# Other places in SBUF for the split weights and the tiles around them

## The chip, the cores and the metric

The kernel runs on one core of a Trainium2 chip. The metric is the time of one execution on the device in microseconds (us): the median of the runs is 1040.94 us before the change (three runs, 1040.69 to 1042.45).

The engines are named as the profile names them: PE (TensorE, matmuls), PEld (its loading of weights), DVE (VectorE), ACT (ScalarE), POOL (GpSimd), SP (SyncE, here an issuer of DMAs).

## What is computed

One layer of a bidirectional encoder: batch 1, sequence 512, width 1024, all in float32. The condition `c` gives nine vectors of shifts, scales and gates.

```python
h = modulate(rmsnorm(x, norm_ffn1), sh1, sc1)
x = x + 0.5 * g1 * swiglu(h, w_ffn1_in, w_ffn1_out)      # FFN1, inner width 2816

h = modulate(rmsnorm(x, norm_mix), sh2, sc2)
qa, ka, va, qb, kb, vb, ga, gb = split(h @ w_in)
ya = window_gqa_sink(rope(qa), rope(ka), va) @ w_branch_a  # 8 heads of 64, 2 of keys, window 128
yb = diff_attention(rope(qb), rope(kb), vb) @ w_branch_b   # 4 heads, two softmaxes each
merged = sigmoid(ga) * ya + sigmoid(gb) * yb
x = x + g2 * (merged @ w_out)

h = modulate(rmsnorm(x, norm_ffn2), sh3, sc3)
x = x + 0.5 * g3 * swiglu(h, w_ffn2_in, w_ffn2_out)      # FFN2
```

## The kernel before

**Three products for one.** A float32 operand is split into a high part, rounded to the type fp32r, and a low part, the rest. A product of two split operands is three matmuls that add up in one bank of PSUM: high by high, high by low, low by high (`mm3`; `two` in the FFNs; L173 to L175 and L456 to L458 in the profile). Each matmul has two operands in SBUF: the **weights**, 128 by 128, which PE loads ahead (PEld), and the **moving** operand, 256 or 512 columns that are streamed past the weights. A row of the profile or of the order of instructions names the tile it writes, an arrow, the moving operand, and the weights: `acc<-b,high` streams an activation in a tile `b` past weights in the tile `high`.

**The stages**, with their times in the profiled execution: the condition, the first norm and a first part of FFN1 (to 82 us), FFN1 (82 to 339 us), the gates of the mixers (to 377 us, and on beside other work), projections and the two attentions (377 to 644 us), the branches and the output product (644 to 729 us), FFN2 (729 to 1038 us). Most of the FFNs' input products are made by `Unit`s: a scheme of Strassen's kind, with seven products, named `a11`, `s1`, `a12`, `a22`, `s4`, `s2` and `s3`, where others would need eight. Each is a group of 24 matmuls or multiples of it with 256 columns. In most groups the moving operand lies in a tile `b`; for `s1` it lies in a tile `u` (rows `acc<-u,low`).

**The places.** Split weights come to lie in two large tiles, `high` and `low`, each with five places of 1024 floats (`HILO`), handed out in turn by `high_low`. The start of a place is `i * 1024 + min(i, 2) * GAP + aside` floats: only the first two places have a gap of 64 floats (256 bytes) behind them, and `aside` shifts the operand inside its place by `ASIDE` (16 floats, 64 bytes), `TURN` (24 floats, 96 bytes), `FAR` (64 floats) or nothing, as the caller asks. The other tiles (`b8`, of which `b` in the profile are parts, `u4`, named `u`, `ka`, `x`, `raw`, `f2`) are laid out in the order in which the kernel first asks for them, so that a small tile ahead of them shifts them.

**What the text counts.** While a matmul streams its moving operand, PE loads the weights of the next one. The *offset* of a pair is the address of the next matmul's weights less that of the current moving operand, modulo 256 bytes. It can be read from the places: `high` begins at 64 modulo 256, `b8` at 64 and `u4` at 160. With `ASIDE` the weights lie at 128, so that a tile `b` gives 64 and a tile `u` gives 224; with `TURN` and a tile `b` it is 96.

**The order of instructions.** The order on each engine is a list scheduler's, which works from modelled costs and sees when an operation overwrites what another still reads; a few stretches are written by hand (`tc.manual_schedule`, `in_order`, `issue_after`). Weights come by DMA, most from SP's queue and a part from POOL's, are split by ACT (the high part) and DVE (the low part), and are then read by PE.

Of the kernel before, what the change touches and what calls it, by code (L numbers as in the profile page):

```python
# [13 lines left out]
I32 = mybir.dt.int32  # L14
# [82 lines left out]

RAW, HILO, F2 = 5, 5, 8

ASIDE, TURN, GAP = 16, 24, 64  # L100

FAR = 64


BRANCH_ASIDES = (ASIDE, TURN, ASIDE, ASIDE), (ASIDE,) * 4
MIX_ASIDES = 0, 0, 0, 0, 0, 0, ASIDE, ASIDE

CHUNKS = (range(0, 6), range(6, 12), range(12, 16), range(16, 22))
# [25 lines left out]
def layer(ctx: ExitStack, tc: tile.TileContext, a: dict):  # L134
# [13 lines left out]
    def xt():  # L148
        return sbuf("x", [P, T], F32, 8)
# [16 lines left out]
    def keep(shape, nm, dt=F32):  # L166
        return sb.tile(shape, dt, name=nm, tag=nm, bufs=1)
# [28 lines left out]
    def high_low(n=1024, aside=0, holder=None):  # L196
        while turn[0] % HILO in holders:
            turn[0] += 1
        i = turn[0] % HILO
        turn[0] += 1  # L200
        if holder:
            holders[i] = holder
        i = i * 1024 + min(i, 2) * GAP + aside
        return tuple(t[:, i : i + n] for t in parts)

    def let_go(holder):
# [24 lines left out]
    sub8, lam_s, nlam = (keep([P, n], nm) for nm, n in (("sub8", 1), ("lam_s", 2), ("nlam", 1)))  # L231
    rqa, ccol = keep([P, NT, 8], "rqa"), small(NC)
    x = [xt() for _ in range(NC)]
    parts, modv = [], []
    for nm, n in (("high", 6), ("low", 0)):
        parts.append(keep([P, HILO * 1024 + 2 * GAP + ASIDE], nm, F32R))
        modv += [keep([P, NC], f"mod{v}") for v in range(n)]

    def load_by(t, src, n):
# [9 lines left out]
        return w  # L249


    begin, begins, norms = keep([P, 6 * NC], "begin"), {}, {SC1: NORM1, SC2: NORM2, SC3: NORM3}

    def mod_begin(v):
        if v in (SH1, SH2, SH3):
# [204 lines left out]
    class Unit:  # L460
# [12 lines left out]
        MAKE = {"s1": 5, "a11": 3, "a12": 2, "s2": 4, "s4": 2, "s3": 2, "a22": 3}  # L473
        asked, length = ("s1", "a11", "a12", "a22"), 1.0

        in_order = turned = ()
        spare, roomy, apart, more = ("s1",), (), (), {"s1": ("s2", "a11"), "s2": ("s4", "a12"), "a11": ("s3", "a21")}

        def place(self, q):
# [14 lines left out]
        def prepare(self, q):  # L494

            if q in self.ready:
                return
            self.ask(q)
            n = self.depth * 2 * P
            if q in self.apart:  # L500
                both = b8().rearrange("p a b -> p (a b)")
                hi, lo = both[:, 0:n], both[:, 1024 : 1024 + n]
            else:
                hi, lo = high_low(n, TURN if q in self.turned else ASIDE, (self, q))
            t = self.at[q]
            with tc.issue_after(copied[0]) if q in self.in_order and copied else nullcontext():
                split_from(hi, lo, t)
            self.ready[q] = hi, lo
            if q in self.more:
                s, src = self.more[q]  # L510
                G.dma_start(t, self.srcs[src], accum_op=ALU.add)
                self.at[s] = t
# [102 lines left out]
    cact = [sbuf("ka", [P, D], F32, 1)]  # L615
    hh, hl = new_h()
    modv += [keep([P, NC], f"mod{v}") for v in range(len(modv), 9)]
    nc.scalar.dma_start(ccol, a["c"])
    tc.keep_in_program_order(nc.scalar.dma_start(par, a["par"]))
    for c in range(NC):  # L620
# [2 lines left out]
    with tc.manual_schedule(engines=BOUND | {mybir.EngineType.SP, mybir.EngineType.Pool}):  # L623
# [24 lines left out]
        def first_loads(k):  # L648
            n = 1 if k else 2
            scale = mod_load(SC1, k, n=n)  # L650
            if k == 0:
                kept.append(keep([P, NT], "pos", I32))
            shift = mod_load(SH1, k, n=n) if k == 0 else None
            raw = sbuf("raw", [P, 1024], F32, RAW)
            load_by(raw, a["w1s"][k], n)
            w1[k] = [scale, shift or mod_load(SH1, k), raw]
# [227 lines left out]
    def in_unit1(p):  # L884
        srcs = {q: a["w1u"][p - PLAIN, i] for i, q in enumerate(("a11", "a12", "a21", "a22"))}
        u = Unit(srcs, 4, h1_operand, in_post1, p % 2)
        u.p, u.in_order = p, ('s2', 's4')
        return u

    class Out1:  # L890
# [17 lines left out]
        def prepare(self, m):  # L908
            if m not in self.ready:
                self.ask(m)  # L910
                aside = FAR if not self.by_halves(m) else TURN if m < NC - LAST_1 + 2 else ASIDE
                if self.final and m == 0:
                    while turn[0] % HILO != 1:
                        turn[0] += 1
                t = self.ready[m] = high_low(self.depth * P, aside, (self, m))
                with tc.issue_after(copied[0]):
                    split_from(*t, self.at[m])
# [279 lines left out]
    def project_pairs(srcs, then):  # L1197

        n = 2 * P
        out = [bank("acc") for _ in range(2)]  # L1200
        for u, src in enumerate(srcs):
            wh, wl = load_main(src, ASIDE)
            for t in range(NT):
                ht = slice(t * P, (t + 1) * P)
                po = out[t // 2][:, t % 2 * n : (t % 2 + 1) * n]
                for i in range(4):
                    k = 4 * u + i
                    w = slice(i * n, (i + 1) * n)
                    first, last = k == 0 and t % 2 == 0, k == NC - 1 and t % 2 == 1
                    PE.matmul(po, hh[k][:, ht], wh[:, w], start=first, stop=False, skip_group_check=True)  # L1210
                    PE.matmul(po, hh[k][:, ht], wl[:, w], start=False, stop=False, skip_group_check=True)
                    PE.matmul(po, hl[k][:, ht], wh[:, w], start=False, stop=last, skip_group_check=True)
                    yield MM3 / 2
        then(out)
# [11 lines left out]
    def gates(more=lambda: True):  # L1226
        while gate_next[0] < 16 and more():
            j = gate_next[0]
            gate_next[0] += 1

            wh, wl = load_main(a["w_gate"][j], ASIDE * (j == EARLY_A))
            out = bank("acc")
            for k in range(NC):
                o = k * P
                mm3(out, wh[:, o : o + P], wl[:, o : o + P], hh[k], hl[k], k == 0, k == NC - 1)
                yield MM3
            gate_end(j, out)
# [423 lines left out]
            turns["w"] = (b, g * nk + kc + 1)  # L1661


    def branch(w, j0, o_h, o_l, then, load, r=FULL[0], asides=(0, 0, 0, 0)):
        for u in range(4):
            with tc.issue_after(banded_last[0]):
                wh, wl = load(w[u], aside=asides[u])
            for i in range(2):
                j = 2 * u + i
                g = f2()[:, r]  # L1670
                nc.sync.dma_start(g, gate_scr[j0 + j][:, r])
                y = bank("acc")[:, r]
                for k in range(4):
                    o = k * 256 + i * P
                    mm3(y, wh[:, o : o + P], wl[:, o : o + P], o_h[:, k, r], o_l[:, k, r], k == 0, k == 3)
                    yield MM3 * (r.stop - r.start) / T
                then(j, g, y, r)

    def main():
        yield from beside(project(vb_w, T, values_b), LATER)  # L1680
        yield from beside(project(a["w_kb"], T, keys_b), LATER)
        yield from beside(project(a["w_qb"], T, queries_b), LATER)
        yield from beside(gates(lambda: gate_next[0] < EARLY_A), 1)
        while later or asked:
            column(later)
        tables_a()
        yield from project_pairs([a["w_kva"][u] for u in range(2)], keys_a)
        for g in range(2):
            yield from project_pairs([a["w_qa"][2 * g + u] for u in range(2)], lambda ps, g=g: queries_a(ps, g))
        yield from gates(lambda: done["b"] < NT)  # L1690
        line.drain(lambda: done["b"] == NT)
        start_a()
        yield from gates()
        ma = [b8(F32) for _ in range(2)]

        def then_a(j, g, y, r):
            V.scalar_tensor_tensor(ma[j // 4][:, j % 4, r], g, 1.0, y, ALU.add, ALU.mult)
            line.helped(0.6)

        yield from branch(a["w_yb"], 8, ob_h, ob_l, then_a, load_main)  # L1700
        mix.extend(new_h())
        mh, ml = mix

        def then_b(j, g, y, r):
            V.scalar_tensor_tensor(g, g, 1.0, y, ALU.add, ALU.mult)
            m = ma[j // 4][:, j % 4, r]
            V.tensor_tensor(m, m, g, ALU.add)
            split_from(mh[j][:, r], ml[j][:, r], m)
            line.helped(1.0)

        for i, r in enumerate(HALVES):
            line.drain(lambda: done["a"] >= 2 * i + 2)
            yield from branch(a["w_ya"], 0, *wa["o"], then_b, load_halves, r, BRANCH_ASIDES[i])

    mix = []
    line.run(main())
# [45 lines left out]

    def in_unit(p):
        srcs = {q: a["w2i"][p, i] for i, q in enumerate(("a11", "a12", "a21", "a22"))}
        return Unit(srcs, 4, h_operand, in_post, p % 2)


    act = {}
# [71 lines left out]
            V.scalar_tensor_tensor(g, g, -1.0, self.bank[1, t], ALU.mult, ALU.mult)  # L1840

    plain = units[0] = Plain(units[0].srcs, 4, h_operand, None, 0)
    plain.turned = ("a11", "a21")
    lead = units[1]
    lead.spare, lead.roomy, lead.apart = ("s1", "a11", "a12"), ("a22",), ("s1", "a12")
    for u in units[1:]:
# [254 lines left out]
```

## Time and profile before

| | before |
|---|---|
| median of three runs | 1040.94 us |
| the profiled execution: its span | 1039.1 us |
| DVE busy | 787.7 us, 76% |
| ACT busy | 583.8 us, 56% |
| DMA moved | 220.92 MB |

The span reaches from the first instruction to the last; the median lies 1.84 us above it. Matmuls are pipelined: the profile gives a matmul from the start of its stream to its modelled end, so that a matmul of 256 columns shows some 0.28 us while the next one starts 0.11 us after it. A difference of a few nanoseconds between two rows of matmuls of one shape is a difference in the distance from start to start:

```profile
start us, us, engine line op out<-in xcount [idle before <-releaser]
652.75 0.28 PE L175 MATMUL acc<-b,low 128*128 128x256 f32 x1
652.86 0.28 PE L173 MATMUL acc<-b,high 128*128 128x256 f32 x1
652.97 0.28 PE L174 MATMUL acc<-b,high 128*128 128x256 f32 x1
653.09 0.28 PE L175 MATMUL acc<-b,low 128*128 128x256 f32 x1
```

The columns are the start, the duration, the engine, the line and the operation.

### The profile page before, as it was taken

How to read it: one execution, taken by the hardware profiler on the slowest of the kernel's cores; microseconds unless marked ns; L12 is line 12 of the kernel's file. 1: busy time of each engine (PE TensorE's matmuls, PEld its weight loads, DVE VectorE, ACT ScalarE, POOL GpSimd, SP SyncE). 2: the span in 40 equal slices, each digit the busy share in tenths (PEclk: the TensorE clock that was granted, in tenths of full speed). 3: DMA queues.
4: the chain of work that ended last, by engine and by line, in shares of the span. 5: the costliest groups of instructions: out<-in, count | busy, mean ns of one | idle time of the engine just before them, and what ended most of it. 6: DMA issues, size and time to landing. Idle time of an engine off the chain costs nothing.

```text
span 1039.1 us, 18835 instructions
## 1 busy us (share of the span) xinstructions
PE 1031.4 (99%) x7346; PEld 952.4 (92%) x7346; DVE 787.7 (76%) x1456; ACT 583.8 (56%) x1014; POOL 162.9 (16%) x190
## 2 busy tenths in 40 slices
PE   9999999999999999999999999999999999999998
PEld 7789899899998998899888888989999999999998
DVE  7786667567796679859772588976899777877867
ACT  6665335244465343667785856525867546655553
POOL 1101110110110100543333101001112112212210
PEclk9999999999999999999999999999999999999999
DMA  9978787967884359796737944974498998989974
GB/s 363 358 233 203 234 231 212 257 160 221 237 203 138 146 201 410 234 286 138 182 71 190 263 129 158 359 248 102 97 237 193 246 225 207 230 221 216 206 149 112
DMA packets 69225, 220.92 MB, mean 213 GB/s; under 512 B 8336, under 2 KB 11024, under 8 KB 69136
## 3 DMA queue, kind: packets, MB, share of 16 engines
q1 hardware_dynamic: 46656, 146.52, 38.8%
q0 software_dynamic: 19344, 68.70, 36.3%
q10 hardware_dynamic: 3136, 4.51, 1.2%
q8 instruction: 57, 0.93, 0.3%
q14 instruction: 32, 0.26, 0.1%
HBM read 209.46 MB, written 10.23 MB: 211 GB/s over the span
## 4 chain that ended last, share of the span: by engine, by line
PE 94%; DMA 2%; DVE 2%; ACT 2%; issue 0%; SPq 0%; DVEq 0%; ACTq 0%
PE acc L457 7%; PE acc L456 7%; PE acc L458 7%; PE sc L456 6%; PE sc L457 6%; PE sc L458 6%; PE sc L173 5%; PE sc L174 5%; PE sc L175 5%; PE acc L173 5%; PE acc L175 5%; PE acc L174 5%; PE tp L1269 2%; DMA raw<-w1s 2%; PE acc L1193 2%; PE acc L1191 2%
## 5 line engine op out<-in xcount | busy, mean ns | idle before, releaser
L189 ACT CAST high<-raw 128x1024 fp32r<-128x1024 f32 (+2 forms) x176 | 158.4, 913 | 150.7 <-PE sc L174 41.1
L189 DVE TENSOR_TENSOR low<-raw,high 128x1024 fp32r<-128x1024 f32 (+2 forms) x176 | 183.5, 1052 | 40.2 <-ACT high L189 38.7
L456 PE MATMUL acc<-b,high 128*128 128x256 f32 x508 | 140.9, 277 | 0.0
L457 PE MATMUL acc<-b,high 128*128 128x256 f32 x508 | 140.8, 277 | 0.1
L458 PE MATMUL acc<-b,low 128*128 128x256 f32 x508 | 140.6, 277 | 0.0
L457 PE MATMUL sc<-b,high 128*128 128x256 f32 x500 | 138.2, 276 | 0.0
L456 PE MATMUL sc<-b,high 128*128 128x256 f32 x500 | 138.2, 276 | 0.0
L458 PE MATMUL sc<-b,low 128*128 128x256 f32 x500 | 138.2, 276 | 0.0
L189 ACT CAST high<-u 128x1024 fp32r<-128x1024 f32 (+1 forms) x73 | 75.5, 1035 | 52.6 <-PE sc L174 20.2
L189 DVE TENSOR_TENSOR low<-u,high 128x1024 fp32r<-128x1024 f32 (+1 forms) x73 | 87.7, 1202 | 21.3 <-ACT high L189 19.6
L173 PE MATMUL sc<-b,high 128*128 128x512 f32 (+1 forms) x272 | 97.5, 358 | 0.0
L174 PE MATMUL sc<-b,high 128*128 128x512 f32 (+1 forms) x272 | 97.1, 357 | 0.0
L175 PE MATMUL sc<-b,low 128*128 128x512 f32 (+1 forms) x272 | 97.1, 357 | 0.0
L457 PEld LDWEIGHTS acc<-b,high 128*128 128x128 f32 x508 | 95.5, 188 | 0.4 <-DVE b L1885 0.3
L456 PEld LDWEIGHTS acc<-b,high 128*128 128x128 f32 x508 | 95.5, 188 | 0.3 <-ACT f L533 0.2
L458 PEld LDWEIGHTS acc<-b,low 128*128 128x128 f32 x508 | 95.4, 188 | 0.0
L456 PEld LDWEIGHTS sc<-b,high 128*128 128x128 f32 x500 | 93.9, 188 | 0.0
L458 PEld LDWEIGHTS sc<-b,low 128*128 128x128 f32 x500 | 93.9, 188 | 0.0
L457 PEld LDWEIGHTS sc<-b,high 128*128 128x128 f32 x500 | 93.9, 188 | 0.0
L173 PE MATMUL acc<-b,high 128*128 128x512 f32 (+1 forms) x240 | 89.0, 371 | 0.0
L175 PE MATMUL acc<-b,low 128*128 128x512 f32 (+1 forms) x240 | 86.7, 361 | 0.0
L174 PE MATMUL acc<-b,high 128*128 128x512 f32 (+1 forms) x240 | 86.6, 361 | 0.0
(397 smaller groups left out, 2720.6 us busy)
## 6 DMA issues: line engine op xcount, KB each, us to landing
u<-w_mod SPq DMA_DIRECT2D x38, 512.0 KB, 8.1
b<-w_mod SPq DMA_DIRECT2D x32, 512.0 KB, 5.7
raw<-w2i SPq DMA_DIRECT2D x31, 512.0 KB, 5.4
u<-w2i POOLq DMA_DIRECT2D x31, 512.0 KB, 7.4
raw<-w1u SPq DMA_DIRECT2D x24, 512.0 KB, 6.4
u<-w1u POOLq DMA_DIRECT2D x24, 512.0 KB, 6.6
raw<-w1o SPq DMA_DIRECT2D x24, 384.0 KB, 4.9
raw<-w_gate SPq DMA_DIRECT2D x16, 512.0 KB, 5.4
```

Of the source, the lines that this page charges most:

```text
L173: PE.matmul(out, wh, xh, start=first, stop=False)
L174: PE.matmul(out, wh, xl, start=False, stop=False)
L175: PE.matmul(out, wl, xh, start=False, stop=last)
L189: last = S.copy(hi, src), V.tensor_tensor(lo, src, f(hi), ALU.subtract)
L456: PE.matmul(out, wh[:, s], xh, start=first and j == 0, stop=False, skip_group_check=True)
L457: PE.matmul(out, wh[:, s], xl, start=False, stop=False, skip_group_check=True)
L458: PE.matmul(out, wl[:, s], xh, start=False, stop=last and j == 1, skip_group_check=True)
L1191: PE.matmul(out[t][:, 0:n], hh[k][:, ht], wh[:, o : o + n], start=k == 0, stop=False)
L1193: PE.matmul(out[t][:, 0:n], hl[k][:, ht], wh[:, o : o + n], start=False, stop=k == NC - 1)
L1269: PE.transpose(tp[:, j * P : (j + 1) * P], src, ident)
```

## The change

No operation of the computation is added or removed. The start of a place becomes `i * (1024 + GAP) + ASIDE + aside`: every place has a gap of 64 floats behind it, and all of them are shifted by 64 bytes. Callers that want something else ask for it: `s1` of the `Unit`s takes no shift of its own (`asides`), the projections take `-ASIDE`. `TURN` and all its uses go. Two small tiles (`pad1`, 192 bytes, and `pad2`, 96 bytes), 16 more floats in `begin` and a larger `pos` shift the tiles behind them. The ring for DMAs that POOL issues shrinks from 4096 to 2048 bytes.

```diff
-ASIDE, TURN, GAP = 16, 24, 64
+ASIDE, GAP = 16, 64
...
-        i = i * 1024 + min(i, 2) * GAP + aside
+        i = i * (1024 + GAP) + ASIDE + aside
...
+    keep([P, 48], "pad1")
...
-        parts.append(keep([P, HILO * 1024 + 2 * GAP + ASIDE], nm, F32R))
+        parts.append(keep([P, HILO * (1024 + GAP) + ASIDE], nm, F32R))
...
-    begin, begins, norms = keep([P, 6 * NC], "begin"), {}, {SC1: NORM1, SC2: NORM2, SC3: NORM3}
+    begin, begins, norms = keep([P, 6 * NC + ASIDE], "begin"), {}, {SC1: NORM1, SC2: NORM2, SC3: NORM3}
...
-                hi, lo = high_low(n, TURN if q in self.turned else ASIDE, (self, q))
+                hi, lo = high_low(n, self.asides.get(q, ASIDE), (self, q))
...
+    keep([P, 24], "pad2")
...
-        u.p, u.in_order = p, ('s2', 's4')
+        u.p, u.in_order, u.asides = p, ('s2', 's4'), {"s1": 0}
...
-                aside = FAR if not self.by_halves(m) else TURN if m < NC - LAST_1 + 2 else ASIDE
+                aside = ASIDE if self.by_halves(m) else FAR
...
-            wh, wl = load_main(src, ASIDE)
+            wh, wl = load_main(src, -ASIDE)
...
-            wh, wl = load_main(a["w_gate"][j], ASIDE * (j == EARLY_A))
+            wh, wl = load_main(a["w_gate"][j])
...
-            yield from branch(a["w_ya"], 0, *wa["o"], then_b, load_halves, r, BRANCH_ASIDES[i])
+            yield from branch(a["w_ya"], 0, *wa["o"], then_b, load_halves, r, ASIDE)
...
+        u.asides = {"s1": 0}
...
-    plain.turned = ("a11", "a21")
...
-    nc = bacc.Bacc("TRN2", target_bir_lowering=False, num_devices=1, dynamic_dma_scratch_size=4096)
+    nc = bacc.Bacc("TRN2", target_bir_lowering=False, num_devices=1, dynamic_dma_scratch_size=2048)
```

The tiles then begin, modulo 256 bytes: `high` and `low` at 0 (before 64), `u4` at 0 (160), `raw` at 64 (192), `f2` at 64 (192); `b8`, `ka` and `x` stay at 64. Counted over all pairs of matmuls that follow one another, by the columns of the first and the offset:

| columns | offset | before | after | which ones |
|---|---|---|---|---|
| 256 | 64 | 3864 | 4944 | most of the FFNs; after, also the projections, `s1` and the attentions' `op<-u,b` |
| 256 | 224 | 458 | 0 | `s1` of the `Unit`s |
| 256 | 96 | 330 | 0 | the first gates; groups with `TURN` |
| 256 | 192 | 278 | 141 | before the projections, after the first gates |
| 256 | 160 | 233 | 0 | the attentions' `op<-u,b` |
| 256 | 128 | 0 | 65 | the last matmul of an `s1` group; short runs of up to six in FFN2, between parts of a group |
| 256 | 0 | 93 | 106 | the last matmul ahead of an `s1` group, and others |
| 512 | 0 | 1608 | 1632 | |
| 512 | 64 | 28 | 5 | a stretch of the attentions; the last matmul ahead of a `Unit` |
| 512 | 96 | 1 | 0 | |

Since fewer operands overlap in the tiles `high` and `low` (before, the last three places lay side by side, so that a shifted operand reached 64 to 96 bytes into the next place), the scheduler has fewer orders to keep, and some instructions move by a row. POOL and SP keep their order. On ACT, where the FFN1 `Unit` at about 61 us has its `s1` weights split (`u` is the arrived tile, `high` the place; `b` and `f` are activations), there stood:

```order
59 L857 ACTIVATE f_86_588<-acc_233 128x512
60 L189 CAST b_83_579<-f_85_583 128x512
61 L189 CAST b_88_592<-f_87_589 128x512
62 L857 ACTIVATE f_89_595<-op_255 128x512
63 L189 CAST high<-u_91_601 128x1024
64 L189 CAST b_88_592<-f_90_596 128x512
```

and now stands:

```order
59 L858 ACTIVATE f_86_590<-acc_235 128x512
60 L188 CAST b_83_581<-f_85_585 128x512
61 L188 CAST high<-u_91_603 128x1024
62 L188 CAST b_88_594<-f_87_591 128x512
63 L858 ACTIVATE f_89_597<-op_257 128x512
64 L188 CAST b_88_594<-f_90_598 128x512
```

The split of the weights moved up by two rows, past one activation and one split of an activation.

On PE, in the projections at about 466 us (`acc` takes a projection, `tp` a transpose, `sc` a product of the attention), there stood:

```order
2857 L1212 MATMUL acc_4520<-high,b_267_3239 128x256
2858 L1210 MATMUL acc_4520<-high,b_265_3237 128x256
2859 L1269 MATMUL tp_4544<-ident,f_404_4256 128x128 x4
2860 L1211 MATMUL acc_4520<-low,b_265_3237 128x256
2861 L1212 MATMUL acc_4520<-high,b_267_3239 128x256
```

and now stands:

```order
2857 L1213 MATMUL acc_4522<-high,b_267_3241 128x256
2858 L1270 MATMUL tp_4546<-ident,f_404_4258 128x128 x4
2859 L1211 MATMUL acc_4522<-high,b_265_3239 128x256
2860 L1212 MATMUL acc_4522<-low,b_265_3239 128x256
2861 L1213 MATMUL acc_4522<-high,b_267_3241 128x256
```

Four transposes moved ahead of one matmul; this is the only difference on PE.

More of the change, by code (lines that the diff above doesn't have):

```diff
@@ L98 @@
 RAW, HILO, F2 = 5, 5, 8
-ASIDE, TURN, GAP = 16, 24, 64
+ASIDE, GAP = 16, 64
 FAR = 64
-BRANCH_ASIDES = (ASIDE, TURN, ASIDE, ASIDE), (ASIDE,) * 4
 MIX_ASIDES = 0, 0, 0, 0, 0, 0, ASIDE, ASIDE
@@ L474, in layer @@
         asked, length = ("s1", "a11", "a12", "a22"), 1.0
-        in_order = turned = ()
+        in_order, asides = (), {}
         spare, roomy, apart, more = ("s1",), (), (), {"s1": ("s2", "a11"), "s2": ("s4", "a12"), "a11": ("s3", "a21")}
@@ L651, in first_loads @@
             if k == 0:
-                kept.append(keep([P, NT], "pos", I32))
+                kept.append(keep([P, 2 * NC], "pos", I32)[:, 0:NT])
             shift = mod_load(SH1, k, n=n) if k == 0 else None
@@ L1661, in window_out, with branch @@
             turns["w"] = (b, g * nk + kc + 1)
-    def branch(w, j0, o_h, o_l, then, load, r=FULL[0], asides=(0, 0, 0, 0)):
+    def branch(w, j0, o_h, o_l, then, load, r=FULL[0], aside=0):
         for u in range(4):
             with tc.issue_after(banded_last[0]):
-                wh, wl = load(w[u], aside=asides[u])
+                wh, wl = load(w[u], aside=aside)
             for i in range(2):
@@ L1764, in in_unit @@
         srcs = {q: a["w2i"][p, i] for i, q in enumerate(("a11", "a12", "a21", "a22"))}
-        return Unit(srcs, 4, h_operand, in_post, p % 2)
+        u = Unit(srcs, 4, h_operand, in_post, p % 2)
+        u.asides = {"s1": 0}
+        return u
     act = {}
```

## The prediction

> **What bounds the kernel now.** I read the page first: which engine is busy, the granted clock, and the chain that ended last.
>
> ```profile
> span 1039.1 us, 18835 instructions
> PE 1031.4 (99%) x7346; PEld 952.4 (92%) x7346; DVE 787.7 (76%) x1456; ACT 583.8 (56%) x1014; POOL 162.9 (16%) x190
> PEclk9999999999999999999999999999999999999999
> PE 94%; DMA 2%; DVE 2%; ACT 2%; issue 0%; SPq 0%; DVEq 0%; ACTq 0%
> ```
>
> PE is busy for 99% of the span, at full clock in every slice, and makes up 94% of the chain. The view of PE's waits says what others can take from it:
>
> ```profile
> PE acc L702 <- ACT b L689: 1.5, 2, 1.0
> PE acc L630 <- DVE sm L636: 0.9, 1, 0.9
> PE op L739 <- POOL sm L735: 0.2, 1, 0.2
> PE acc L186 <- DVE u L189: 0.2, 1, 0.2
> ```
>
> These are all its waits, 2.8 us in the whole span. The time is therefore the number of matmuls times the distance from one start to the next, and a change of places can act only on that distance. So I read groups of matmuls by form. First FFN2, from 746.2 to 1038 us (line, output<-moving operand, weights, shapes, count | busy us, mean ns | idle):
>
> ```profile
> L456 PE MATMUL acc<-b,high 128*128 128x256 f32 x316 | 87.3, 276 | 0.0
> L457 PE MATMUL sc<-b,high 128*128 128x256 f32 x300 | 82.9, 276 | 0.0
> L456 PE MATMUL op<-b,high 128*128 128x256 f32 x62 | 17.1, 276 | 0.0
> L456 PE MATMUL tp<-b,high 128*128 128x256 f32 x62 | 17.1, 276 | 0.0
> L458 PE MATMUL acc<-u,low 128*128 128x256 f32 x48 | 13.4, 280 | 0.0
> L458 PE MATMUL sc<-u,low 128*128 128x256 f32 x40 | 11.2, 280 | 0.0
> ```
>
> One shape has two durations: 276 ns where the offset is 64 (moving operand in `b`), 280 where it is 224 (in `u`). That is what the change is about, 4 ns in 276. Then I looked at short windows, one row of each, in order of time: 142.3 to 145.1, 315.7 to 323.2, 649 to 651.6, 651.8 to 668, 723.8 to 729, 729.3 to 732, 732.2 to 737.5 and 737.8 to 743 us:
>
> ```profile
> L458 PE MATMUL acc<-b,low 128*128 128x256 f32 x8 | 2.2, 281 | 0.0
> ...
> L457 PE MATMUL acc<-b,high 128*128 128x256 f32 x22 | 6.2, 281 | 0.0
> ...
> L174 PE MATMUL acc<-b,high 128*128 128x256 f32 x8 | 2.2, 280 | 0.0
> ...
> L174 PE MATMUL acc<-b,high 128*128 128x256 f32 x49 | 13.5, 276 | 0.0
> ...
> L457 PE MATMUL acc<-b,high 128*128 128x256 f32 x15 | 4.2, 281 | 0.0
> ...
> L456 PE MATMUL acc<-b,b 128*128 128x256 f32 x8 | 2.3, 283 | 0.0
> ...
> L456 PE MATMUL sc<-b,high 128*128 128x256 f32 x16 | 4.5, 280 | 0.0
> ...
> L457 PE MATMUL sc<-b,high 128*128 128x256 f32 x17 | 4.7, 276 | 0.0
> ```
>
> By the places, their offsets are 64, 64, 96, 64, 64, 0, 96 and 64. So **offset 64 has two prices**: 276 in the fourth and last row, 281 in the first, second and fifth. Offset 0 costs 283, offset 96 costs 280. I call 276 the *settled* state and 281 the *unsettled*. Behind a block of 512 columns (first row) a run is unsettled and stays so; each run of 276 here stands behind a group of another offset (the fourth behind the third, the last behind the seventh). Traffic isn't the cause, as the view by windows has it (PE busy, clock, DMA share, GB/s):
>
> ```profile
> 315.70:323.20 7.50, 7.50 (x65) 1.00 0.53 157
> 746.20:1038.00 291.80, 288.21 (x2533) 1.00 0.87 204
> ```
>
> The slow stretch has less DMA beside it than the fast one.
>
> **The change part by part.** The `s1` groups of FFN2 (`acc<-u` and `sc<-u`, three lines each) go from offset 224 to 64: 3 x (48 + 40) = 264 matmuls. From 280 to 276, less half a nanosecond since one line of each three shows 279, this is 264 x 3.5 = **0.92 us** less. FFN1 from 82 to 315 us has six more groups, of which one row and, for later use, the rows fed from `b`, and one of 512 columns:
>
> ```profile
> L174 PE MATMUL sc<-b,high 128*128 128x512 f32 x129 | 50.2, 389 | 0.0
> L457 PE MATMUL sc<-b,high 128*128 128x256 f32 x160 | 44.2, 276 | 0.0
> L456 PE MATMUL acc<-b,high 128*128 128x256 f32 x138 | 38.2, 277 | 0.0
> L457 PE MATMUL sc<-u,high 128*128 128x256 f32 x32 | 9.0, 280 | 0.0
> ```
>
> They are 6 x 32 = 192 matmuls by 3.6 = **0.69 us** less. Then the gates (339.7 to 376.6 us), the projections (456 to 499), the attentions' products with `u` (499 to 648), and a stretch of 512 columns at offset 64 (502 to 506.3):
>
> ```profile
> L174 PE MATMUL acc<-b,u 128*128 128x256 f32 x48 | 13.5, 281 | 0.0
> L174 PE MATMUL sc<-b,high 128*128 128x256 f32 x48 | 13.4, 280 | 0.0
> ...
> L1211 PE MATMUL acc<-low,b 128*128 128x256 f32 x92 | 25.8, 280 | 0.0
> ...
> L174 PE MATMUL op<-u,b 128*128 128x256 f32 x67 | 18.9, 282 | 0.0
> ...
> L175 PE MATMUL acc<-b,low 128*128 128x512 f32 x6 | 2.4, 395 | 0.0
> ```
>
> Gates: half of the 288 stay away from 64 (the first gates, 96 to 192; the projections show what 192 costs, 280, so nothing). Of all that may settle I take a third of 288 by 4.5 = **0.43 us**. Projections: 276 matmuls from 192 to 64; transposes break them up, and a broken run may well be unsettled, which costs 281 instead of 280. Bounds: 276 x 4 = 1.1 us less if all settle, 0.3 more if none does; I take a third settled, **0.37 us**. Products with `u`: 202 from offset 160; bounds 202 x 6 = 1.2 and 202 x 1 = 0.2 less; a third settled gives **0.54 us**. The stretch of 512 columns shows 395 ns where offset 0 showed 389 (the first row of FFN1 above); pairs at 64 go from 28 to 5, so 23 x 6 = **0.14 us** less. At FFN2's start the 48 matmuls at 280 may keep 280 or go to 276, half of 0.19: **0.10 us**.
>
> What is added: in each `s1` group the single pair ahead of it is at offset 0 (283 by the row above, 7 over 276) and the last one at 128, which no row of before shows. Pairs at 0 go from 93 to 106, so 13 x 7 = 0.09 us; the 65 at 128 cost between nothing (as 276) and what offset 0 costs, 65 x 7 = 0.46. I take the middle: together **0.3 us** more.
>
> Moved rows and the ring: the splits that move on ACT are near these rows of its timeline, and POOL's queue has these:
>
> ```profile
> 61.42 1.04 ACT L189 CAST high<-u 128x1024 fp32r<-128x1024 f32 x1
> ...
> POOL u L511 <- DVE low L189: 278.9, 42, 56.4
> ...
> u<-w2i POOLq DMA_DIRECT2D x31, 512.0 KB, 7.4
> ```
>
> A split of 1.04 us comes two rows earlier, so an activation behind it 1.04 us later; PE waits for ACT 1.5 us in all, in the first product of FFN1 (L702), which stands ahead of that place, so I cost it at nothing. Without that cover it would be up to 1.04 us once. On PE one matmul changes sides with four transposes: the same work. A ring of half the size could at worst make POOL wait before it issues; it already waits 278.9 us for room in `u`, and a transfer that lands in 7.4 us is issued that much ahead, so I cost it at nothing.
>
> Sum: 0.92 + 0.69 + 0.43 + 0.37 + 0.54 + 0.14 + 0.10 − 0.3 = 2.9 us less. Against the profiled execution 1039.1 becomes 1036.2; the median lies 1.84 us above that span, which gives **1038.0 us**.
>
> [...]
>
> **The rivals.**
>
> *The unsettled state stays* (slower). Settled runs of before stand behind groups at 224 or 96, and the change takes just these groups away: in FFN1 and FFN2 nothing but 64 is left, with single pairs at 0 and 128. If a run begins unsettled behind the 512-column block or behind the 24 matmuls at 283 (729.3 us), and a single other pair doesn't turn it, it stays at 281. In FFN2 3 x (316 + 300 + 62 + 62) = 2220 matmuls by 5 are 11.1 us more; the `s1` groups go to 281 too, so their 0.92 is lost, and 1 ns each is added, 0.3. FFN1 has 3 x (160 + 138) = 894, of which 72 are unsettled already: 822 by 5 = 4.1 us more. With FFN2 alone: 1040.94 + 11.1 + 0.3 − 0.69 − 1.3 (the rest of the sum) = **1050.4 us**; with both, 1055. It decides at the first pairs of each stage: one that settles behind its first `s1` group costs under 0.5 us. For it: 315.7 to 323.2 us, 65 matmuls that never settle of themselves. Against it: the stretch at 651.8 us holds 276 for 146 matmuls and FFN2 for 2220 without falling back.
>
> *Gains given back* (no change). `s1` settles, but the single pairs knock a part of the runs out: 2.9 us less against some 550 matmuls by 5 = 2.75 more. That gives **1040.8 us**.
>
> [...]
>
> *The order or the ring counts*: one activation late by 1.04 us on PE's path, or POOL late at the 42 transfers, gives 1039 to 1042.
>
> **How the numbers follow.** The forecast gets 0.42: its largest terms need only that `s1` behaves as its neighbours do. The unsettled state gets 0.34, given back 0.17, no matter 0.05, order and ring 0.02. The forecast's own range is 1034.5 (all bounded terms at their ends: gates 1.3, projections 1.1, products 1.2, and the unsettled stretches of before, 315.7 us and FFN1's starts, settled) to 1039.5. To leave out no more than 2 in 10, the range goes on over "given back" and most of the slower rival: 1034.5 to 1052, leaving out FFN1 and FFN2 both unsettled. A measurement of this kernel can tell about 0.2% from no change, 2.1 us: faster is below 1038.9, slower above 1043.0. Faster 0.43, of the forecast and a little of the last rival; slower 0.34; the rest, 0.23, the same.
>
> **What would show it.** Right: `acc<-u` and `sc<-u` in FFN2 at 276, `acc<-b` there still 276, `op<-u,b` at 276 to 281. Wrong: `acc<-b,high` at 281 in FFN2 or in stretches of FFN1 (the rival), `acc<-u` at 280 (no matter), or PE's waits well over 2.8 us (order).

## The result, and the profile after

The changed kernel takes 1050.49 us (median of five executions, 1050.33 to 1052.19), the kernel before 1041.05 us beside it. The ratio is 1.0091, with a 95% interval of 1.008 to 1.0102: slower by 9.4 us. The forecast was 1038.0.

The page of the changed kernel, its first lines and the chain that ended last, and then the view of PE's waits:

```profile
span 1048.6 us, 18834 instructions
PE 1041.5 (99%) x7346; PEld 962.5 (92%) x7346; DVE 788.2 (75%) x1456; ACT 584.0 (56%) x1014; POOL 163.0 (16%) x190
...
PEclk9999999999999999999999999999999999999999
...
PE 94%; DMA 2%; DVE 2%; ACT 1%; issue 0%; SPq 0%; DVEq 0%; ACTq 0%
```

```profile
PE acc L703 <- ACT b L690: 1.1, 2, 0.8
PE acc L631 <- DVE sm L637: 0.9, 1, 0.9
PE acc L185 <- DVE u L188: 0.2, 1, 0.2
```

PE has the same 7346 matmuls and 10.1 us more of busy time, at full clock, and waits 2.2 us where it waited 2.8. Nothing became late: the matmuls themselves stand farther apart. FFN2 by form, 746.2 to 1048 us:

```profile
L456 PE MATMUL acc<-b,high 128*128 128x256 f32 x316 | 88.7, 281 | 0.0
L457 PE MATMUL sc<-b,high 128*128 128x256 f32 x300 | 83.6, 279 | 0.0
L456 PE MATMUL op<-b,high 128*128 128x256 f32 x62 | 17.4, 281 | 0.0
L456 PE MATMUL tp<-b,high 128*128 128x256 f32 x62 | 17.3, 278 | 0.0
L458 PE MATMUL acc<-u,low 128*128 128x256 f32 x48 | 13.4, 279 | 0.0
L458 PE MATMUL sc<-u,low 128*128 128x256 f32 x40 | 11.2, 280 | 0.0
```

The long runs, all at 276 ns before and still at offset 64, went to 281, or to a mean between 276 and 281; the `s1` rows, for which the change was to pay, stayed at 279 to 280. Where the time went, by the starts of the same matmul in the two traces, subtracted stage by stage:

| stage (times of before) | before, us | after less before, us |
|---|---|---|
| FFN1, 82.2 to 339.7 | 257.5 | +3.64 |
| gates, to 376.7 | 37.0 | −0.11 |
| projections, 454.4 to 499.4 | 45.1 | −0.53 |
| attentions, to 644.6 | 145.2 | −0.68 |
| branches, to 668.2 | 23.5 | +0.60 |
| FFN2's start, 700.4 to 746.1 | 45.7 | +0.15 |
| FFN2, to the start of the last matmul | 288.0 | +7.20 |

The stages left out add 0.02 us together, and the part ahead of 82.2 us, with PE's waits, −0.67. What loses most is where runs were settled before; what gains is where they were broken up by transposes or stood at 160 and 192.

The loss of the FFNs can be added up. Of the long runs' pairs at 64 in FFN2, 42 of 2265 stood 116 ns or more apart before and 1690 of 2259 after; 1648 more by 4.5 ns are 7.4 us. In FFN1 it is 156 of 1146 before and 1070 of 1139 after, 914 more by 4.5, or 4.1 us. The `s1` groups give a little of that back, 0.1 us in FFN2 and 0.4 in FFN1.

Windows around two `s1` groups of FFN2 show where the runs change. In order of time, 743.0 to 745.8, 746.1 to 748.5, 748.8 to 756.9, 757.3 to 759.7 and 760 to 776.6 us:

```profile
L456 PE MATMUL sc<-b,high 128*128 128x256 f32 x8 | 2.2, 281 | 0.0
...
L456 PE MATMUL tp<-u,b 128*128 128x256 f32 x7 | 1.9, 276 | 0.0
...
L457 PE MATMUL acc<-b,high 128*128 128x256 f32 x8 | 2.2, 281 | 0.0
...
L456 PE MATMUL acc<-u,high 128*128 128x256 f32 x7 | 1.9, 276 | 0.0
...
L456 PE MATMUL acc<-b,high 128*128 128x256 f32 x24 | 6.7, 281 | 0.0
```

The two `s1` groups are settled, the runs ahead of and behind them are not. Into each of the two leads one pair at offset 0, out of it one at 128. Other `s1` groups of FFN2 are fed in pieces, with six pairs in a row at 128. The run ahead of the first of these is unsettled, and what follows is settled for most of the time until 874 us (823 to 835.2, and 841.7 to 854.4 us):

```profile
L456 PE MATMUL acc<-b,high 128*128 128x256 f32 x23 | 6.5, 281 | 0.0
...
L456 PE MATMUL sc<-b,high 128*128 128x256 f32 x25 | 6.9, 276 | 0.0
```

So a quarter of FFN2's runs stays settled after the change. The theory to test is **A: a run at offset 64 goes on in the state it begins in, and what stands ahead of it, be it one pair, sets that state; 0 turns an unsettled run, 128 unsettles.** Rivals: **B**, the smaller ring or the order of instructions; **C**, the `TURN` groups that are gone, so that no stage ever settles; **D**, an unsettled run settles of itself, and it is any break that costs the state.

### The profile page after: what moved, and what is told of

It is laid out like the page before. It is cut to its first block, busy times and chain, and to the rows that moved or that the text cites. A ratio compares the mean times of both kernels' runs of the same rounds, so it can differ in the third digit from the quotient of the medians.

```text
span 1048.6 us, 18834 instructions
## 1 busy us (share of the span) xinstructions
PE 1041.5 (99%) x7346; PEld 962.5 (92%) x7346; DVE 788.2 (75%) x1456; ACT 584.0 (56%) x1014; POOL 163.0 (16%) x190
## 4 chain that ended last, share of the span: by engine, by line
PE 94%; DMA 2%; DVE 2%; ACT 1%; issue 0%; SPq 0%; DVEq 0%; ACTq 0%
PE acc L457 7%; PE acc L458 7%; PE acc L456 7%; PE sc L458 6%; PE sc L457 6%; PE sc L456 6%; PE sc L172 5%; PE sc L174 5%; PE sc L173 5%; PE acc L172 5%; PE acc L173 5%; PE acc L174 5%; PE tp L1270 2%; PE acc L1192 2%; PE acc L1194 2%; PE acc L1193 2%
## 5 line engine op out<-in xcount | busy, mean ns | idle before, releaser
L188 DVE TENSOR_TENSOR low<-raw,high 128x1024 fp32r<-128x1024 f32 (+2 forms) x176 | 183.2, 1050 | 42.1 <-ACT high L188 40.4
L456 PE MATMUL acc<-b,high 128*128 128x256 f32 x508 | 142.8, 281 | 0.0
L457 PE MATMUL acc<-b,high 128*128 128x256 f32 x508 | 142.7, 281 | 0.1
L456 PE MATMUL sc<-b,high 128*128 128x256 f32 x500 | 139.8, 280 | 0.0
L457 PE MATMUL sc<-b,high 128*128 128x256 f32 x500 | 139.8, 280 | 0.0
L173 PE MATMUL sc<-b,high 128*128 128x512 f32 (+1 forms) x272 | 97.2, 357 | 0.0
L173 PE MATMUL acc<-b,high 128*128 128x512 f32 (+1 forms) x240 | 86.7, 361 | 0.0
```

Source lines behind the costliest of these rows:

```text
L173: PE.matmul(out, wh, xl, start=False, stop=False)
L188: last = S.copy(hi, src), V.tensor_tensor(lo, src, f(hi), ALU.subtract)
L456: PE.matmul(out, wh[:, s], xh, start=first and j == 0, stop=False, skip_group_check=True)
L457: PE.matmul(out, wh[:, s], xl, start=False, stop=False, skip_group_check=True)
```

## Experiments

Where a diff below shows `u.asides` of the `Unit`s once, it is FFN2's; FFN1's `Unit`s get the same value in a line of their own (`u.p, u.in_order, u.asides = ...`).

### The ring alone (`e1_ring`)

```diff
-    nc = bacc.Bacc("TRN2", ..., dynamic_dma_scratch_size=4096)
+    nc = bacc.Bacc("TRN2", ..., dynamic_dma_scratch_size=2048)
```

on the kernel before.

> The kernel of before with one part of the change alone: the ring for POOL's DMAs at 2048 bytes instead of 4096, all places as before. Theory A (the single pairs that lead into and out of the s1 groups decide in which of two states the long runs at offset 64 go on): no effect, 1041 us, rows acc<-b,high and sc<-b,high in FFN2 at 276 ns. Rival B (the smaller ring delays POOL's transfers): toward 1050 us, with waits on PE and matmuls still at 276.

1041.13 us against 1041.24; ratio 1.0001 (0.9992 to 1.0011). The ring costs nothing, B's first half falls. Its second half falls with the runs below: but for the next one, they have exactly the changed kernel's order of instructions on every engine, and take from 1038.6 to 1055.3 us.

### The `s1` groups alone (`e5_s1alone`)

The kernel before, `TURN` groups and all, with the smaller ring and `u` at 0:

```diff
+    keep([P, 24], "pad2")
...
-        hi, lo = high_low(n, TURN if q in self.turned else ASIDE, (self, q))
+        hi, lo = high_low(n, TURN if q in self.turned else self.asides.get(q, ASIDE), (self, q))
...
+        u.asides = {"s1": 0}
```

Here some `s1` weights begin where a shifted operand in the place ahead still lies, so the last 16 columns of that operand are overwritten and a part of the FFNs' products takes other weights. The matmuls are as many as before, 7346.

> The kernel of before (its places, TURN groups and asides), with the ring of 2048 bytes and only the s1 groups moved as in the change: tile u at 0 modulo 256, s1 weights without a shift, so that inside an s1 group the offset is 64, the pair ahead of it is at 0 and its last at 128. Some rows of FFN1 trade places on PE. Theory A: nearly all of the loss is there, 1048 to 1051 us, with acc<-b,high in FFN2 at 281 and sc at 279. Rival C (the loss comes from the TURN groups at 96 that are gone at the starts of stages, after which nothing settles): FFN2 keeps its 96 group here, settles behind it and stays at 276, so 1039 to 1041 us.

1052.63 us; ratio 1.0112 (1.0097 to 1.0127), a little more than expected: FFN2 loses the same 7.20 us as in the changed kernel, FFN1 4.97, and the projections gain 0.05 where the changed kernel gains 0.53. By form, windows of FFN2: 737 to 740 (the `TURN` group), 744 to 746.3, 746.8 to 749 (`s1` begins), and 748 to 1050 us:

```profile
L456 PE MATMUL sc<-b,high 128*128 128x256 f32 x9 | 2.5, 280 | 0.0
...
L457 PE MATMUL sc<-b,high 128*128 128x256 f32 x8 | 2.2, 276 | 0.0
...
L456 PE MATMUL tp<-u,b 128*128 128x256 f32 x4 | 1.1, 282 | 0.0
...
L456 PE MATMUL acc<-b,high 128*128 128x256 f32 x316 | 88.7, 281 | 0.0
L456 PE MATMUL sc<-b,high 128*128 128x256 f32 x300 | 83.6, 279 | 0.0
```

The `TURN` group is there, the run behind it is settled, and the first `s1` group ends that. Its last two rows are the 281 and 279 of the changed kernel. C falls for FFN2. It also showed that offset 0 doesn't only settle: ahead of this group the run was settled, and behind the pair at 0 it no longer was.

### `s1` back at 224 (`e3_u160`)

The changed kernel with `u` at 160 again:

```diff
-    keep([P, 24], "pad2")
...
-        u.asides = {"s1": 0}
+        u.asides = {"s1": ASIDE}
```

> The changed kernel with one part undone: tile u back at 160 modulo 256 (pad2 left out) and the s1 weights with their shift, so that s1 groups are again 24 matmuls at offset 224; the TURN groups stay away, gaps and ring stay as changed. Theory A: the long runs settle behind each s1 group, FFN2 rows acc<-b,high and sc<-b,high at 276, s1 rows at 280, 1039 to 1041.5 us. Rival C: FFN2 stays unsettled from its start, 281, about 1050 us.

1040.87 us; ratio 0.9998 (0.9988 to 1.0007). FFN2 from 746 us on:

```profile
L456 PE MATMUL acc<-b,high 128*128 128x256 f32 x315 | 87.0, 276 | 0.0
L457 PE MATMUL sc<-b,high 128*128 128x256 f32 x300 | 82.9, 276 | 0.0
...
L458 PE MATMUL acc<-u,low 128*128 128x256 f32 x48 | 13.4, 280 | 0.0
```

With the gaps, the smaller ring and no `TURN`, the loss is gone as soon as the `s1` groups stand at another offset for 24 matmuls. By the starts of matmuls its FFN1 is within 0.3 us of before, FFN2 within 0.3.

### The two single pairs traded (`e2_u128`)

```diff
-    keep([P, 24], "pad2")
+    keep([P, 56], "pad2")
...
-        u.asides = {"s1": 0}
+        u.asides = {"s1": 2 * ASIDE}
```

> The changed kernel with tile u at 128 modulo 256 (pad2 larger) and the s1 weights at 192: inside an s1 group the offset is still 64, but the pair ahead is now at 128 and its last at 0, the two of the change traded. Theory A, if 0 settles and 128 unsettles: the long runs behind s1 at 276, the s1 groups at 280 to 281, 1039 to 1042 us. If any single pair breaks the settled state, about 1050 us as the change. Rival C: about 1050 us.

1042.41 us; ratio 1.0014 (1.0004 to 1.0023), 0.4 above the range expected. Two windows of FFN2, an `s1` group (755.1 to 757.6) and a run behind another (874.2 to 890.1):

```profile
L457 PE MATMUL acc<-u,high 128*128 128x256 f32 x7 | 2.0, 281 | 0.0
...
L456 PE MATMUL acc<-b,high 128*128 128x256 f32 x32 | 8.8, 276 | 0.0
```

In FFN2 this is the picture of the changed kernel with the two states exchanged: `s1` unsettled, the long runs settled but for 71 of 2253 pairs. In FFN1 it holds for half: 577 of 1139 are unsettled there, and the stage is 1.81 us above before, half of the changed kernel's 3.64. The same number of single pairs, the same breaks, 8.1 us less: against the half of D by which any break costs the state, this is the decisive pair of runs.

### Nothing but 64 (`e6_u64`)

```diff
-    keep([P, 24], "pad2")
+    keep([P, 40], "pad2")
...
-        u.asides = {"s1": 0}
+        u.asides = {"s1": ASIDE}
```

> The changed kernel with tile u at 64 modulo 256 (pad2 larger) and the s1 weights with their shift: no single pairs are left, and FFN2 from its second group on is 2532 matmuls at offset 64 without a break; the order of instructions is that of the changed kernel. Theory A (a run keeps the state it begins in): FFN2 begins unsettled behind 24 matmuls at offset 0, so all of it stays at 281, s1 rows too, and FFN1's runs also; 1051 to 1054 us, above the change. Rival D (an unsettled run settles of itself after some hundred matmuls, and it was the single pairs that kept throwing it out): 276 in most of FFN2, about 1038 us.

1055.28 us; ratio 1.0127 (1.011 to 1.0145), the slowest of all and 1.3 above the range expected. FFN2 from 750.8 to 1052 us:

```profile
L456 PE MATMUL acc<-b,high 128*128 128x256 f32 x316 | 88.8, 281 | 0.0
L457 PE MATMUL sc<-b,high 128*128 128x256 f32 x300 | 84.3, 281 | 0.0
L456 PE MATMUL acc<-u,high 128*128 128x256 f32 x48 | 13.5, 281 | 0.0
```

2532 matmuls in a row at the offset that has the best price, all at the worse of its two. The other half of D falls: nothing settles of itself in 300 us.

### Nothing but 64, and groups that settle (`e7_settle`)

On top of the last one:

```diff
-        u.p, u.in_order, u.asides = p, ('s2', 's4'), {"s1": ASIDE}
+        u.p, u.in_order, u.asides = p, ('s2', 's4'), {3: {"s1": -8}, 4: {"s2": -8}, 6: {"s2": -8}, 8: {"s2": -8}}.get(p, {})
...
-                wh, wl = load(w[u], aside=aside)
+                wh, wl = load(w[u], aside=-8 if aside and not u else aside)
...
-        u.asides = {"s1": ASIDE}
+        u.asides = {2: {"a11": -8}}.get(p, {})
...
+    plain.asides = {"a11": -8}
```

> As e6_u64, and one group in each stretch given weights shifted to 32 modulo 256, that is offset 224 for 24 matmuls (48 in FFN2's first part, and the first branch weights): the first group of each FFN1 stage, the a11 of FFN2's third unit. Same order of instructions. Theory A with offset 224 as what settles: everything behind these groups at 276 to the stage's end, FFN2 2508 matmuls with s1 rows at 276; 1038.5 to 1040 us, below before. Rival D: no gain over e6_u64, since the groups would only break runs.

Of twelve executions ten took 1037.94 to 1040.07 us and two took 1048.58 and 1049.12; the median is 1038.87, the ratio 0.9987 (0.9966 to 1.0009). The execution that was profiled has a span of 1046.8 us, like the two, and shows why. FFN2, by form from 747.6 to 764 and from 770 to 1045 us, then its timeline between (start, duration), and the view by windows (length, PE busy, clock, DMA share, GB/s):

```profile
L456 PE MATMUL sc<-b,high 128*128 128x256 f32 x17 | 4.7, 276 | 0.0
...
L456 PE MATMUL sc<-b,high 128*128 128x256 f32 x276 | 77.6, 281 | 0.0
```

```profile
766.33 0.28 PE L458 MATMUL sc<-b,low 128*128 128x256 f32 x1
766.44 0.34 PE L456 MATMUL acc<-b,high 128*128 128x256 f32 x1
766.62 0.28 PE L457 MATMUL acc<-b,high 128*128 128x256 f32 x1
```

```profile
747.60:764.00 16.40, 16.40 (x147) 1.00 1.01 228
770.00:1045.00 275.00, 272.26 (x2312) 1.00 0.83 197
```

One matmul at 766.44 us stands 0.18 us from the next instead of 0.11, a hitch of some 65 ns, and the 2300 behind it are unsettled to the end. That single hitch costs some 10 us, and no group at 224 follows in FFN2. The DMAs are busier in the settled stretch than in the other one (a share of 1.01 against 0.83), as in the kernel before (0.87 against 0.53). So half of the expectation held: the group settles, but "to the stage's end" only where nothing disturbs it. (The execution of 1049.12 us has no trace.)

Other traces have hitches too, and not every one does this. The same matmul is 31 ns late in the trace of before, and its run stays settled; with the ring alone, two starts there stand 263 and 226 ns apart, and the next 48 matmuls are unsettled, until a group at 224. Near the end of FFN1 all twelve traces have a hitch, of 249 to 275 and then 220 ns or a little more between starts. It can also turn the state the other way. In the changed kernel the run ahead of it is unsettled (303 to 318.3 us) and the one behind it settled (319.6 to 326.5 us):

```profile
L456 PE MATMUL sc<-b,high 128*128 128x256 f32 x18 | 5.1, 281 | 0.0
...
318.44 0.28 PE L458 MATMUL acc<-b,low 128*128 128x256 f32 x1
318.69 0.38 PE L456 MATMUL acc<-b,high 128*128 128x256 f32 x1
318.91 0.29 PE L457 MATMUL acc<-b,high 128*128 128x256 f32 x1
...
L456 PE MATMUL acc<-b,high 128*128 128x256 f32 x20 | 5.5, 276 | 0.0
```

Of eight settled runs ahead of this hitch it left three unsettled, before's among them (the row of 315.7 us in the prediction); four unsettled ones it settled.

### Other pairs around `s1` (`e4_u160w`, `e8_u192`)

The changed kernel with `u` at 160 and `s1` weights at 224 (pairs at 160 ahead, 224 last), and with `u` at 192 and weights at 0 (192 both times):

```diff
-    keep([P, 24], "pad2")
...
-        u.asides = {"s1": 0}
+        u.asides = {"s1": 40}
```

```diff
-    keep([P, 24], "pad2")
+    keep([P, 8], "pad2")
...
-        u.asides = {"s1": 0}
+        u.asides = {"s1": 48}
```

> The changed kernel with tile u at 160 (pad2 left out) and s1 weights at 224: inside an s1 group offset 64, the pair ahead of it at 160, its last at 224. Same order of instructions. Theory A says only that the two offsets decide; if one pair at 224 settles as a group of 24 does, the long runs are at 276, and 1039 to 1041 us; if it does nothing or unsettles, 1045 to 1052 us. If any break of a run costs the state, about 1050 us.

> As e4_u160w with tile u at 192 and s1 weights at 256, that is 0: offset 64 inside, 192 both ahead and last. Same order of instructions. Theory A: the state behind each pair follows from the state ahead of it and the offset 192, the same way in every unit; no forecast of which way, 1039 to 1052 us. If any break of a run costs the state, about 1050 us.

The first takes 1039.6 us, ratio 0.9984 (0.9975 to 0.9993), and FFN2's rows from 746 us on are the best so far, `s1` with them:

```profile
L456 PE MATMUL acc<-b,high 128*128 128x256 f32 x313 | 86.5, 276 | 0.0
L457 PE MATMUL sc<-b,high 128*128 128x256 f32 x300 | 82.9, 276 | 0.0
...
L457 PE MATMUL acc<-u,high 128*128 128x256 f32 x48 | 13.3, 277 | 0.0
L457 PE MATMUL sc<-u,high 128*128 128x256 f32 x40 | 11.1, 277 | 0.0
```

The second takes 1046.76 us, ratio 1.0047 (1.0033 to 1.0061). It is mixed, against "the same way in every unit": 748 to 870 us, and 876 to 1043:

```profile
L456 PE MATMUL acc<-b,high 128*128 128x256 f32 x120 | 33.7, 281 | 0.0
...
L456 PE MATMUL acc<-b,high 128*128 128x256 f32 x196 | 54.1, 276 | 0.0
```

Over the traces of before, after and the experiments but the first and the repeat I counted what a pair does: the state of at least ten matmuls at 64 ahead of it (by their last six) and of at least twelve behind it (by the sixth to eleventh), settled where starts lie under 115 ns apart:

| offset, how many | from unsettled | from settled |
|---|---|---|
| 0, one | 35 of 35 settle | 10 of 10 unsettle |
| 128, one | 7 of 18 settle | 33 of 33 unsettle |
| 160, one | 4 of 4 settle | 21 of 21 stay settled |
| 192, one | 12 of 21 settle | 10 of 10 unsettle |
| 224, one | none seen | 34 of 34 stay settled |
| 224, twelve or more | 7 of 7 settle | 27 of 27 stay settled |

This bears out A and mends its wording: a pair at 0 doesn't settle, it exchanges the two states. The counts are of places in ten kernels that share most of their order, and not of independent trials. Runs of five or six pairs are not in the table, and do otherwise: six in a row at 128 left all 12 runs behind them settled, five unsettled 4 of 4.

### The two that work, together (`e9_both`, and `e10_u160w2`)

The kernel with 160 and 224 around `s1`, and groups at 224 at the starts of the later FFN1 stages, in the first branch weights and in FFN2's first part and third unit (edits as above); beside it the former once more.

> e4_u160w (single pairs at 160 and 224 around each s1 group) and groups at offset 224 at the starts of the later FFN1 stages, of the first branch weights and in FFN2's first part and third unit, as in e7_settle. Same order of instructions. Theory A: what e4_u160w left unsettled settles too: three runs of 23 in FFN1 (0.3 us), the branch run of 173 at 117.8 (0.8 us less the cost of its groups), FFN2's first runs of 96 and 71 (0.5 us); and since each unit has a pair that settles, no execution stays unsettled for long, as one of e7_settle can: 1038 to 1039 us, all executions within 3 us. Rival D: no difference from e4_u160w, 1039.6 us.

> e4_u160w once more, beside e9_both on one chip: 1039.6 us; sc and acc rows of FFN2 at 276, s1 rows at 276, all by theory A.

1038.63 us (1038.18 to 1038.99, five executions), ratio 0.9965 (0.9952 to 0.9979), against 1039.6 us, 0.9983 (0.9974 to 0.9991), for the former alone, whose `s1` rows stand at 276 to 278. The branch run (650 to 666 us) is at 277, where the changed kernel has 281 (650.2 to 670.4); the changed kernel's row comes second:

```profile
L173 PE MATMUL acc<-b,high 128*128 128x256 f32 x48 | 13.3, 277 | 0.0
```

```profile
L173 PE MATMUL acc<-b,high 128*128 128x256 f32 x58 | 16.3, 281 | 0.0
```

It beats the kernel before by 2.6 us beside it, and the changed one by 11.9 across two sets of runs, with the changed kernel's order of instructions throughout. None of its five executions had the jump of 10 us; five are few to rule it out.

## Why the prediction was wrong

**The bound** was right: PE at 99%, waits of 2.2 us after, and every microsecond of the difference in the distance of matmuls.

**The step that failed** is the price of what is added. The sum took the single pairs at 0 and 128 by their own duration, "together 0.3 us more". A pair's own duration is of little matter here; what it costs is the state that it leaves to the run behind it. The 128 pairs unsettled 14 of 14 settled runs in the changed kernel's trace, and 71 to 306 matmuls stand behind each. For these long runs the sum had no term at all: it left them at 276, and they cost 7.4 us more in FFN2 and 4.1 in FFN1. The bound was wrong too: it was drawn from rows of the pair (0 to 7 ns) when the trace had already shown two prices of one offset that last, and it showed no row for offset 128 at all.

**Term by term.** `s1` in FFN2, 0.92 us less forecast, 0.10 measured: single groups did reach 276 (757.3 us), while those that began settled were unsettled by their own pair at 0, and those fed in pieces have pairs at 128 between the parts, at some 119 ns. `s1` in FFN1, 0.69 forecast, 0.43 measured. Projections, 0.37 forecast, 0.53 measured. Attentions, 0.54 and 0.14 forecast, 0.68 measured. Gates, 0.43 forecast, 0.11 measured. FFN2's start, 0.10 less forecast, 0.15 more measured; the branches, not in the sum, 0.60 more.

**The rival** *the unsettled state stays* had named the row to look at (`acc<-b,high` at 281) and a time, 1050.4 us, that is the measured one; the stated range reaches the measurement only because it was drawn over this rival. The agreement is partly luck: it laid 11.4 us on FFN2 and nothing on FFN1 and the branches, and measured were 7.2, 3.6 and 0.6. Its mechanism was half right. Runs do keep their state (2532 at 281), runs do begin unsettled behind 512 columns (281 at 142.3 us of before), and with the groups at 224 back (`e3_u160`) the loss is gone. But it held that the single pairs might fail to turn the state; in the run with the `TURN` group kept, and in the changed kernel's own windows, pairs turned it both ways, and the wrong way ahead of the long runs. And a kernel without these groups can be as good as before, with other single pairs (`e4_u160w`). The evidence for this rival, 65 matmuls at 315.7 us "that never settle of themselves", is right as far as it goes, but what unsettled them was a hitch: the run of 149 pairs ahead of it was settled.

**Places of no matter**, with 0.05 of the chances: the runs don't bear this out. Kernels with one order of instructions, which differ in places alone, took from 1038.63 to 1055.28 us, and `acc<-b,high` in FFN2 stands at 276 in one of them and at 281 in another (`e3_u160`, `e6_u64`).

**The order and the ring** cost nothing, as forecast: 1041.13 us against 1041.24 with the ring alone, and 1040.87 with the changed kernel's order, its ring and `s1` back at 224.

**Open:** what the two states are; no run shows it. A hitch of 65 ns turned one (`e7_settle`), a pair turns one (the table above), and DMA traffic doesn't follow them: the settled stretch has the larger share of DMA in `e7_settle` (1.01 against 0.83) and in the kernel before (0.87 against 0.53). Why 128 settles 7 of 18 unsettled runs and 192 12 of 21 is open too; it suggests that the price alone doesn't tell the whole state. So is why six pairs in a row at 128 settle where one unsettles, and what makes a hitch turn a run or leave it. What the new places of `raw` and `f2` do by themselves wasn't tried: they move together with `u`. The two kernels with `u` at 64 (`e6_u64`, `e7_settle`) have them at the same places and lie 16.4 us apart, so they aren't what parts these two.

## What to carry to other kernels

When one shape shows two durations at one and the same setting, find what stands ahead of each stretch before a change is priced: an inserted or removed operation is then worth the state that it leaves behind, times all that follows (here 4.5 ns on each of 71 to 306 matmuls), and not its own duration. Make the common case uniform only together with something that sets it right, again and again: the uniform kernel was the slowest here (1055.28 us), and where one group was to settle a whole stage, two of twelve executions took 10 us more, the traced one after a single hitch. Kernels that differ only in addresses, with one order of instructions, tell such causes apart stage by stage, by the starts of the same matmuls, within some tenths of a microsecond.

## What the runs showed of the hardware

In the kernel before, the load of the next weights begins with the current matmul: PEld L173 and PE L175 both at 652.75 us, the load 0.19 us long, the next matmul at 652.86. For fp32r matmuls of 256 columns the distance from start to start went with the offset and with what had run ahead: 113.3 ns settled (FFN2 of before) and 117.8 unsettled (the changed kernel, 760 to 776.6 us) at offset 64, 120.0 over a group at 0 (before, from 729.3 us); the profile's rows are 276, 281 and 283. The rows went with the difference and not with one address: pairs at 64 had both with `u` at 0 (276 in the changed kernel at 757.3 us, 281 and 282 in `e5_s1alone` at 746.8 us) and at 64 (276 and 281 in `e7_settle`), and 281 with `u` at 128 (`e2_u128`, 755.1 us). At 192 one group of 11 in `e2_u128` stood at 113.5 ns, the settled distance of offset 64. The unsettled state lasted over 2532 matmuls in `e6_u64`. One hitch of 65 ns ended a settled run in `e7_settle`; longer ones turned runs both ways, 274 ns between two starts to unsettled (before, 315.2 us) and 249 to settled (the changed kernel, 318.4 us).
